# Separate buffers in the expert_v stage, and a recurrent scan issued by pairs of heads

## The chip, the cores and the metric

The kernel runs on one core of one Trainium2 chip. The metric is the device time of one execution in microseconds (us). Three runs of the kernel before took 2474.93, 2481.82 and 2487.04 us. The engines are TensorE (PE, with PEld for its weight loads), VectorE (DVE), ScalarE (ACT), GpSimd (POOL) and SyncE (SP), each of which works through its own instructions in order; SP and POOL also issue the DMA transfers.

## What is computed

The reference runs two transformer blocks over one sequence of 512 tokens with 1024 features, in fp32. Cut to what matters here:

```
# first block, mixer: 4 heads of a gated delta rule, 4 heads of sparse attention
for c in 8 chunks of 64 tokens:                       # per head, state 128x128
    v_new = u[c] - w[c] @ state
    o[c]  = q_dec[c] @ state + a[c] @ v_new
    state = state * g_last[c] + k_dec[c].T @ v_new
o_n = attention(q, compressed / selected / window keys)  # in blocks of 128 queries
x = x + gate1 * concat(o_g, o_n) @ w_out              # then a gated feed-forward layer

# second block, last part: 16384 experts, each one row of expert_u and of expert_v
experts, gate = top 16 of 16384 for each token and each of 8 heads
act = gelu(expert_u[experts] . h)
x = x + gate2 * sum(gate * act * expert_v[experts])
return rmsnorm(x, final_g)
```

## The kernel before

One program in which a scheduler orders each engine's instructions from the order in which they are written (their priority), from buffers that come free and from an estimate of durations; the order is then fixed. Every tile name has a number of buffers; a new tile of a name waits until the oldest is released by all its readers, and a pool that is opened takes memory that earlier pools give up, so its tiles wait for these. The large matrix products run on float32r operands that are split in two: `split` (L192 to L194) casts a tile to a high part on ScalarE and subtracts it on VectorE for the low part, and three products (high times high, high times low, low times high) are summed in PSUM.

**First block** (`block1`, from L401). After gates, keys and the inverse of each head's triangular matrix, the loop over the four heads projects q and v (`proj_qv`: a product with 24 matmuls of 512 columns for each, a causal convolution on VectorE, a norm) and finishes the head's scan inputs (`gdn_fin`, PSUM bank 0). Attention blocks 0 and 1 (`nsa`, 128 queries each, all four heads) are written behind heads 0 and 1. Then follows the scan (`gdn_scan`, L738): 8 steps over 64 tokens, all four heads in a step. A step takes the state times w into PSUM bank 0, subtracts on VectorE (L753), multiplies with the keys into bank 1, scales and adds the state on VectorE (L759, L760), and makes the outputs in bank 0 again (two products of 64 columns per head, each of which the trace shows as two records), which ScalarE copies out (L765). Behind the scan are written the four gate projections (`proj_gz`) and attention blocks 2 and 3. A block with `last` false uses banks 2 and 3 for scores, 4 for transposes and bank 1 for its outputs (L896); with `last` true it uses the accumulation banks, 2 to 5. The attention outputs are copied at L907.

**Second block, last part** (`peer`, L1057). The tokens fall into two shares. For the first 384, all 16384 experts are computed densely, 128 at a time: the U stage multiplies expert_u tiles with the normed input (`run_ahead`), applies gelu and writes the activations of 113 of the 128 tiles to DRAM (`spill`). A routing stage and a spreading stage (`spread`) build the gate table, 11 of 12 parts in DRAM (`gdram`) and the last in memory (`glast`); U products fill in beside them. For the last 128 tokens, the 128 (head, choice) slots are gathered instead: one indirect DMA on POOL fetches a row of expert_u or expert_v for each token, 512 KB in all, and VectorE forms a dot product (L1181) or adds up (L1191).

The **last stage** (V, L1121 to L1161) loops over the 128 expert tiles: load the activations back (`pact`, 4 buffers, SP), multiply by the gate table (`gtile`, 4 tiles to a load of 704 KB; L1139 for 11 parts, L1140 for the last), split them (`pwh`, `pwl`), load 512 KB of expert_v (`raw`, SP), split it (`vh`, `vl`, 4 pairs in a pool that is opened with this stage), then gather and add one slot (`gather_sum(1)`), then 24 matmuls of 384 columns into 8 banks. The last three tiles are done together at the end. `ulane` is a ring of 6 `row` buffers with 3 split pairs, made for expert_u; in this stage the V tiles use its 6 buffers, and so do the gathers (`self.row = ulane[0]`, L1112). Of the 128 gathers, the first are issued in the spreading stage, so the last tiles have none.

Of the kernel before, what the change touches and what calls it, by code (L numbers as in the profile page):

```python
# [9 lines left out]
F32 = mybir.dt.float32  # L10
F32R = mybir.dt.float32r
# [139 lines left out]
class Builder:  # L151
# [248 lines left out]
    def block1(self):  # L400
        A, V, x = self.A, self.V, self.x  # L401
        with ExitStack() as st1:
# [55 lines left out]
            with ExitStack() as st2:  # L458
# [15 lines left out]
                self.nsa_begin(kp)  # L474
                for h in range(4):
                    self.proj_qv(h, hi, lo)
                    self.gdn_fin(h)
                    if h < 2:
                        self.nsa(kp, h, False)
                self.gdn_scan()  # L480
                for h in range(4):
                    if h % 2:
                        self.nsa(kp, 2 + h // 2, True)
                    self.proj_gz(h, hi, lo)
            hst.close()
# [234 lines left out]
    def gdn_fin(self, h):  # L720
# [3 lines left out]
        psq = self.ps(0)  # L724
# [7 lines left out]
        ps = self.ps(0)  # L732
# [5 lines left out]
    def gdn_scan(self):  # L738
        V, C, gi = self.V, self.C, self.gi
        wT, at, qd, kd = self.wT, self.at, self.qd, self.kd  # L740
        St = gi.tile([P, 4, P], F32, name="w0", bufs=2)
        V.memset(St, 0.0)
        oT = self.eq
        for c in range(8):
# [4 lines left out]
            psv = self.ps(0)  # L749
            for h in range(4):  # L750
                self.mm(psv[:, h * P:(h + 1) * P], wT[h][:, tb], St[:, h, :])
            vnew = gi.tile([P, 4, P], F32, name="w1", bufs=2)
            V.tensor_tensor(vnew[r], self.kA[r, :, tb], psv[r].rearrange("p (h d) -> p h d", h=4), ALU.subtract)  # L753
            if c < 7:
                psS = self.ps(1)
                for h in range(4):
                    self.mm(psS[:, h * P:(h + 1) * P], kd[h][r, t, :], vnew[r, h, :])
                Sn = gi.tile([P, 4, P], F32, name="w0", bufs=2)
                V.tensor_tensor(Sn, St, self.gl[:, c, :].unsqueeze(2).to_broadcast([P, 4, P]), ALU.mult)  # L759
                V.tensor_tensor(Sn, Sn, psS.rearrange("p (h d) -> p h d", h=4), ALU.add)  # L760
            pso = self.ps(0)
            for h in range(4):
                self.mm(pso[:, h * P:h * P + 64], St[:, h, :], qd[h][:, cs], True, False)
                self.mm(pso[:, h * P:h * P + 64], vnew[r, h, :], at[h][r, t, o:o + 64], False, True)
            C.copy(oT[:, :, cs], pso.rearrange("p (h b) -> p h b", h=4)[:, :, 0:64])  # L765
            if c < 7:
                St = Sn
        self.oT = oT
# [574 lines left out]
```

## Time and profile before

| what | value |
|---|---|
| runs | 2474.93, 2481.82, 2487.04 us |
| profiled execution | 2477.21 us, span 2475.1 us |
| TensorE busy | 2378.9 us, 96%, 12749 matmuls |
| TensorE weight loads | 2150.7 us, 87% |
| VectorE, ScalarE, GpSimd busy | 1843.3 us (74%), 1077.1 us (44%), 337.5 us (14%) |
| TensorE clock granted, mean | 0.977 |
| DMA | 509.40 MB, mean 206 GB/s; 134.23 MB of it indirect (GpSimd's queue) |
| chain of waits by engine | PE 58%, DVE 13%, DMA 13%, issue 7%, ACT 6%, POOL 2% |

Matmuls are pipelined and their ends are modelled, so TensorE shown as busy is not TensorE at its peak: a stretch at half clock is also "busy". What a stage could gain is therefore read from the number of matmuls that it gets through, its clock, and the waits that interrupt it. "issue" in the chain is time without a wait that the profile shows.

### The profile page before, as it was taken

How to read it: one execution, taken by the hardware profiler on the slowest of the kernel's cores; microseconds unless marked ns; L12 is line 12 of the kernel's file. 1: busy time of each engine (PE TensorE's matmuls, PEld its weight loads, DVE VectorE, ACT ScalarE, POOL GpSimd, SP SyncE). 2: the span in 40 equal slices, each digit the busy share in tenths (PEclk: the TensorE clock that was granted, in tenths of full speed). 3: DMA queues.
4: the chain of work that ended last, by engine and by line, in shares of the span. 5: the costliest groups of instructions: out<-in, count | busy, mean ns of one | idle time of the engine just before them, and what ended most of it. 6: DMA issues, size and time to landing. Idle time of an engine off the chain costs nothing.

```text
span 2475.1 us, 35106 instructions
## 1 busy us (share of the span) xinstructions
PE 2378.9 (96%) x12749; PEld 2150.7 (87%) x12749; DVE 1843.3 (74%) x3826; ACT 1077.1 (44%) x1753; POOL 337.5 (14%) x284
## 2 busy tenths in 40 slices
PE   7999999899999999998999999999998999899998
PEld 7788787678878777877899999999998999899997
DVE  6774635788874389665999999899876777787764
ACT  4534624343332233334323334499995333333332
POOL 0000000000000000000232331233101222223310
PEclk9999989899999999998999999999998999999999
DMA  7341102566554222225478897689867999899981
GB/s 276 125 133 60 52 9 85 170 198 193 188 183 144 81 90 92 70 86 188 148 239 291 319 369 259 202 320 345 321 228 244 301 312 311 301 330 327 325 266 52
DMA packets 197934, 509.40 MB, mean 206 GB/s; under 512 B 20352, under 2 KB 93312, under 8 KB 195840
## 3 DMA queue, kind: packets, MB, share of 16 engines
q1 hardware_dynamic: 160896, 372.92, 44.4%
q0 software_dynamic: 36864, 134.23, 15.3%
q8 instruction: 100, 1.64, 0.3%
q14 instruction: 74, 0.61, 0.1%
HBM read 459.71 MB, written 47.38 MB: 205 GB/s over the span
## 4 chain that ended last, share of the span: by engine, by line
PE 58%; DVE 13%; DMA 13%; issue 7%; ACT 6%; POOL 2%; POOLq 0%; DVEq 0%; SPq 0%; ACTq 0%
PE p L162 38%; PE acc L162 19%; DMA row<-in_ev_dram,eidx 7%; DMA raw<-in_ada_dram 2%; ACT o L1296 1%; POOL row L1174 1%; ACT gstage L1304 1%; DVE grow L1181 1%; DVE pN L1191 1%; DVE wlo L194 1%; DMA araw<-in_ada_dram 1%; DVE vl L194 1%; DMA pact<-spill 1%; ACT rowhi L193 1%; DVE rowlo L194 1%
## 5 line engine op out<-in xcount | busy, mean ns | idle before, releaser
L193 ACT CAST whi<-raw 128x1024 fp32r<-128x1024 f32 (+2 forms) x152 | 150.7, 993 | 386.7 <-PE p L162 239.1
L162 PE MATMUL p<-pwl,vh 128*128 128x384 f32 x768 | 262.7, 342 | 25.0 <-DVE pwl L194 24.5
L162 PE MATMUL p<-pwh,vh 128*128 128x384 f32 x768 | 258.3, 338 | 5.2 <-ACT pwh L193 5.2
L162 PE MATMUL p<-pwh,vl 128*128 128x384 f32 x768 | 259.2, 338 | 0.0
L194 DVE TENSOR_TENSOR wlo<-raw,whi 128x1024 fp32r<-128x1024 f32 (+2 forms) x152 | 174.8, 1151 | 102.9 <-ACT whi L193 100.5
L193 ACT CAST vh<-row 128x1024 fp32r<-128x1024 f32 x128 | 134.3, 1051 | 257.3 <-PE acc L162 186.1
L1174 POOL DMA_INDIRECT row<-in_ev_dram,eidx x128 | 161.1, 1259 | 501.5 <-DVE pN L1191 188.4
L1191 DVE SCALAR_TENSOR_TENSOR pN<-row,dots,pN 128x1024 f32<-128x1024 f32 x127 | 162.7, 1281 | 84.9 <-DMA row<-in_ev_dram,eidx 84.6
L193 ACT CAST rowhi<-row 128x1024 fp32r<-128x1024 f32 x128 | 134.5, 1051 | 206.4 <-PE acc L162 94.6
L194 DVE TENSOR_TENSOR rowlo<-row,rowhi 128x1024 fp32r<-128x1024 f32 x128 | 155.8, 1218 | 35.6 <-ACT rowhi L193 35.5
L162 PE MATMUL p<-hi,rowhi 128*128 128x384 f32 x512 | 174.6, 342 | 3.2 <-ACT hi L301 2.6
L162 PE MATMUL p<-lo,rowhi 128*128 128x384 f32 x512 | 175.5, 343 | 1.8 <-DVE lo L302 1.8
L162 PEld LDWEIGHTS p<-pwl,vh 128*128 128x128 f32 x768 | 146.0, 190 | 35.8 <-DVE pwl L194 35.6
L162 PE MATMUL acc<-lo,rowhi 128*128 128x384 f32 x512 | 175.2, 342 | 0.0
L162 PE MATMUL acc<-hi,rowlo 128*128 128x384 f32 x512 | 174.8, 342 | 0.3 <-DVE rowlo L194 0.3
L162 PE MATMUL acc<-hi,rowhi 128*128 128x384 f32 x512 | 174.5, 341 | 0.6 <-ACT rowhi L193 0.6
L162 PE MATMUL p<-hi,rowlo 128*128 128x384 f32 x512 | 174.9, 342 | 0.1
L194 DVE TENSOR_TENSOR vl<-row,vh 128x1024 fp32r<-128x1024 f32 x128 | 155.9, 1219 | 24.7 <-ACT vh L193 24.7
L162 PE MATMUL p<-hi,whi 128*128 128x512 f32 x416 | 164.8, 402 | 5.7 <-ACT hi L301 4.3
L162 PE MATMUL p<-hi,wlo 128*128 128x512 f32 x416 | 166.8, 401 | 1.1 <-DVE wlo L194 1.0
L162 PE MATMUL p<-lo,whi 128*128 128x512 f32 x416 | 165.6, 399 | 0.9 <-DVE lo L302 0.9
L162 PEld LDWEIGHTS p<-pwh,vh 128*128 128x128 f32 x768 | 145.8, 190 | 5.6 <-ACT pwh L193 5.5
(525 smaller groups left out, 6055.0 us busy)
## 6 DMA issues: line engine op xcount, KB each, us to landing
row<-in_eu_dram SPq DMA_DIRECT2D x128, 512.0 KB
row<-in_ev_dram SPq DMA_DIRECT2D x128, 512.0 KB
araw<-in_ada_dram SPq DMA_DIRECT2D x64, 512.0 KB
raw<-in_up_dram SPq DMA_DIRECT2D x44, 512.0 KB
gdram<-gstage SPq DMA_DIRECT2D x11, 2048.0 KB
gtile<-gdram SPq DMA_DIRECT2D x31, 704.0 KB
spill<-pact SPq DMA_DIRECT2D x113, 192.0 KB
pact<-spill SPq DMA_DIRECT2D x113, 192.0 KB
```

Of the source, the lines that this page charges most:

```text
L162: self.T.matmul(out, lhsT, rhs, start=start, stop=stop)
L193: self.C.copy(hi, src)
L194: self.V.tensor_tensor(lo, src, hi.bitcast(F32), ALU.subtract)
L1174: self.G.indirect_dma_start(out=u, out_offset=None, in_=self.A[src], in_offset=bass.IndirectOffsetOnAxis(ap=self.eidx[:, s:s + 1], axis=0))
L1181: self.V.scalar_tensor_tensor(u, u, 1.0, self.hN, ALU.mult, ALU.mult, accum_out=self.dots[:, s:s + 1])
L1191: self.V.scalar_tensor_tensor(self.pN, v, w, self.pN, ALU.mult, ALU.add)
L1296: C.activation(o2[:, i, :], self.iota, AF.Abs, bias=T3[:, 1, t:t + 1])
L1304: C.copy(gs[:, :, q * 4:q * 4 + 4].rearrange("p a t -> p t a"), ps.rearrange("p (t a) -> p t a", t=4))
```

## The change

In the last stage the gathered rows get a name and 6 buffers of their own (`grow`), the V tiles keep the ring of 6, and the spilled activations come into 6 new buffers (`vact`) instead of 4 (`pact`) shared with the U stage. The split V weights rotate through the U stage's three pairs and one new pair, four as before. In the first block the scan is called for heads 0 and 1 behind their projections, and for heads 2 and 3 behind theirs; a step's v product, state product and outputs all lie in bank 0 (two halves), and `gdn_fin` moves to bank 4. All four attention blocks are written behind the second scan, each after one gate projection.

```diff
@@ -472,16 +472,14 @@
                 self.proj_nq(hi, lo)
                 kp = self.pool(st2, "nt")
                 self.nsa_begin(kp)
+                for pair in ((0, 1), (2, 3)):
+                    for h in pair:
+                        self.proj_qv(h, hi, lo)
+                        self.gdn_fin(h)
+                    self.gdn_scan(pair)
                 for h in range(4):
-                    self.proj_qv(h, hi, lo)
-                    self.gdn_fin(h)
-                    if h < 2:
-                        self.nsa(kp, h, False)
-                self.gdn_scan()
-                for h in range(4):
-                    if h % 2:
-                        self.nsa(kp, 2 + h // 2, True)
                     self.proj_gz(h, hi, lo)
+                    self.nsa(kp, h, h > 1)
             hst.close()
             op = self.pool(st1, "op", side="right")
             mh = self.mh = op.tile([P, KD, S], F32R, name="mh")
@@ -721,7 +719,7 @@
         V, C = self.V, self.C
         r4 = lambda v: v.rearrange("p a b -> p (a b)")
         q, k, vN, E, X = self.qT[h], self.kT[h], self.vN[h], self.at[h], self.X[h]
-        psq = self.ps(0)
+        psq = self.ps(4)
         for t in range(TT):
             b = slice(t * P, (t + 1) * P)
             self.mm(psq[:, b], k[:, b], q[:, b])
@@ -729,43 +727,45 @@
         V.tensor_tensor(q, q, self.eq[:, h, :], ALU.mult)
         self.qd.append(q)
         V.tensor_tensor(vN, vN, self.rn[:, h, :].unsqueeze(2).to_broadcast([P, TT, P]), ALU.mult)
-        ps = self.ps(0)
+        ps = self.ps(4)
         for t in range(TT):
             self.mm(ps[:, t * P:(t + 1) * P], X[:, t, :], vN[:, t, :])
         C.copy(k, ps)
 
 
-    def gdn_scan(self):
+    def gdn_scan(self, pair):
         V, C, gi = self.V, self.C, self.gi
         wT, at, qd, kd = self.wT, self.at, self.qd, self.kd
-        St = gi.tile([P, 4, P], F32, name="w0", bufs=2)
+        h0 = pair[0]
+        hs = slice(h0, h0 + 2)
+        new = lambda k: gi.tile([P, 4, P], F32, name=f"w{k}", bufs=2)[:, 0:2, :]
+        St = new(0)
         V.memset(St, 0.0)
-        oT = self.eq
+        oT = self.oT = self.eq
+        half = lambda ps, i: ps[:, i * 2 * P:(i + 1) * 2 * P]
         for c in range(8):
             t, o = divmod(c * 64, P)
             r = slice(o, o + 64)
             tb = slice(t * P, (t + 1) * P)
             cs = slice(c * 64, c * 64 + 64)
-            psv = self.ps(0)
-            for h in range(4):
-                self.mm(psv[:, h * P:(h + 1) * P], wT[h][:, tb], St[:, h, :])
-            vnew = gi.tile([P, 4, P], F32, name="w1", bufs=2)
-            V.tensor_tensor(vnew[r], self.kA[r, :, tb], psv[r].rearrange("p (h d) -> p h d", h=4), ALU.subtract)
+            ps = self.ps(0)
+            psv, psS = half(ps, 0), half(ps, 1)
+            for i, h in enumerate(pair):
+                self.mm(psv[:, i * P:(i + 1) * P], wT[h][:, tb], St[:, i, :])
+            vnew = new(1)
+            V.tensor_tensor(vnew[r], self.kA[r, hs, tb], psv[r].rearrange("p (h d) -> p h d", h=2), ALU.subtract)
             if c < 7:
-                psS = self.ps(1)
-                for h in range(4):
-                    self.mm(psS[:, h * P:(h + 1) * P], kd[h][r, t, :], vnew[r, h, :])
-                Sn = gi.tile([P, 4, P], F32, name="w0", bufs=2)
-                V.tensor_tensor(Sn, St, self.gl[:, c, :].unsqueeze(2).to_broadcast([P, 4, P]), ALU.mult)
-                V.tensor_tensor(Sn, Sn, psS.rearrange("p (h d) -> p h d", h=4), ALU.add)
-            pso = self.ps(0)
-            for h in range(4):
-                self.mm(pso[:, h * P:h * P + 64], St[:, h, :], qd[h][:, cs], True, False)
-                self.mm(pso[:, h * P:h * P + 64], vnew[r, h, :], at[h][r, t, o:o + 64], False, True)
-            C.copy(oT[:, :, cs], pso.rearrange("p (h b) -> p h b", h=4)[:, :, 0:64])
+                for i, h in enumerate(pair):
+                    self.mm(psS[:, i * P:(i + 1) * P], kd[h][r, t, :], vnew[r, i, :])
+                Sn = new(0)
+                V.tensor_tensor(Sn, St, self.gl[:, c, hs].unsqueeze(2).to_broadcast([P, 2, P]), ALU.mult)
+                V.tensor_tensor(Sn, Sn, psS.rearrange("p (h d) -> p h d", h=2), ALU.add)
+            for i, h in enumerate(pair):
+                self.mm(psv[:, i * P:i * P + 64], St[:, i, :], qd[h][:, cs], True, False)
+                self.mm(psv[:, i * P:i * P + 64], vnew[r, i, :], at[h][r, t, o:o + 64], False, True)
+            C.copy(oT[:, hs, cs], psv.rearrange("p (h b) -> p h b", h=2)[:, :, 0:64])
             if c < 7:
                 St = Sn
-        self.oT = oT
 
     def gdn_out(self):
         V, C, G, gp, oT = self.V, self.C, self.G, self.gp, self.oT
@@ -1122,6 +1122,9 @@
                 bank = [self.ps(m) if m < 6 else self.acc() for m in range(KD)]
                 self.sqp = (wk, 4)
                 part = []
+                pair = lambda: [wk.tile([P, D], F32R, name=n, bufs=1) for n in ("vh", "vl")]
+                vring = ulane[1] * LAST + [pair]
+                self.row = lambda: wk.tile([P, D], F32, name="grow", bufs=6)
                 for e in range(P):
                     if e == 0 or e % GA == 2:
                         n, e0 = min(GA, P - e) if e else 2, e
@@ -1131,7 +1134,7 @@
                             gt = self.hN[:, :(NB - 1) * n * TB].rearrange("p (b a t) -> p b a t", b=NB - 1, a=n)
                         self.dma(gt, gd[:, :, e:e + n, :].rearrange("b p a t -> p b a t"))
                     if e < KEPT:
-                        act = ra.tile([P, ND], F32, name="pact", bufs=4)
+                        act = wk.tile([P, ND], F32, name="vact", bufs=6)
                         self.dma(act, sp[e])
                     else:
                         act = kept[e]
@@ -1143,8 +1146,8 @@
                     self.split(wh, wl, act)
                     raw = ulane[0]()
                     self.dma(raw, A["ev"][e * P:(e + 1) * P, :])
-                    vh = wk.tile([P, D], F32R, name="vh", bufs=LAST + 1)
-                    vl = wk.tile([P, D], F32R, name="vl", bufs=LAST + 1)
+                    vring.append(vring.pop(0))
+                    vh, vl = vring[-1]()
                     self.split(vh, vl, raw)
                     part.append((e, wh, wl, vh, vl))
                     self.gather_sum(1)
```

## Rows read from the trace of the kernel before

**Rows 1.** The page's chain of waits, share of the span by engine and line.
```profile
...
PE p L162 38%; PE acc L162 19%; DMA row<-in_ev_dram,eidx 7%; DMA raw<-in_ada_dram 2%; ACT o L1296 1%; POOL row L1174 1%; ACT gstage L1304 1%; DVE grow L1181 1%; DVE pN L1191 1%; DVE wlo L194 1%; DMA araw<-in_ada_dram 1%; DVE vl L194 1%; DMA pact<-spill 1%; ACT rowhi L193 1%; DVE rowlo L194 1%
...
```

**Rows 2.** Busy time of each engine in stretches of the last stage.
```profile
core 0: us, PE busy (x) PEld busy (x) DVE busy (x) ACT busy (x) POOL busy (x), PEclk, DMA share, GB/s
1884.00:2391.00 507.00, 482.04 (x2688) 471.15 (x2689) 379.44 (x561) 169.55 (x225) 137.04 (x106) 0.98 0.91 311
2181.00:2248.00 67.00, 67.00 (x389) 67.00 (x388) 53.55 (x80) 23.91 (x32) 17.83 (x16) 1.00 0.96 338
2391.00:2458.00 67.00, 67.00 (x391) 66.78 (x390) 35.73 (x48) 22.83 (x32) 0.00 (x0) 1.00 0.27 86
```

**Rows 3.** Waits in the last stage; us in total, times, longest us.
```profile
PE p L162 <- DVE pwl L194: 24.5, 25, 2.4
...
DVE pN L1191 <- DMA row<-in_ev_dram,eidx: 76.1, 50, 5.7
...
DVE pact L1139 <- DMA pact<-spill: 48.3, 39, 2.9
...
POOL row L1174 <- DVE pN L1191: 174.6, 58, 7.3
...
```

**Rows 4.** Busy time of each engine, first block, around the scan.
```profile
...
290.00:320.00 30.00, 26.32 (x144) 19.83 (x142) 15.39 (x53) 10.76 (x34) 0.00 (x0) 0.89 0.06 18
320.00:400.00 80.00, 80.00 (x392) 63.85 (x391) 29.20 (x74) 21.99 (x53) 0.00 (x0) 0.81 0.04 14
...
```

**Rows 5.** Busy time of each engine in the expert_u stage.
```profile
...
1420.00:1460.00 40.00, 40.00 (x230) 40.00 (x229) 40.00 (x89) 13.47 (x19) 18.00 (x15) 1.00 1.01 385
...
```

**Rows 6.** Order of time, start of the last stage; start us, us, instruction.
```profile
1870.25 0.38 SPq L1132 DMA_DIRECT2D hN<-gdram  x1
...
1874.24 0.96 DVE L1139 TENSOR_TENSOR pact<-pact,hN 128x352 f32<-128x352 f32 x2 [2.12 <-DMA hN<-gdram]
...
1878.71 1.01 ACT L1304 COPY glast<-p 128x512 f32<-128x512 f32 x1 [0.69 <-PE p L162]
...
1879.53 3.88 ACT L193 CAST vh<-row 128x1024 fp32r<-128x1024 f32 x4
...
1879.76 0.49 DVE L1140 TENSOR_TENSOR pact<-pact,glast 128x32 f32<-128x32 f32 x4 [4.56 <-ACT glast L1304]
...
1883.31 0.93 ACT L193 CAST pwh<-pact 128x384 fp32r<-128x384 f32 x2
...
1883.87 2.29 PE L162 MATMUL p<-pwh,vh 128*128 128x384 f32 x6 [5.19 <-ACT pwh L193]
...
```

**Rows 7.** Loads of spilled activations: duration ns, first and last start.
```profile
...
L1135 SPq DMA_DIRECT2D pact<-spill x113: 319/338/1537, 1769.5 to 2370.5; - x113
...
```

**Rows 8.** Order of time: one scan step (a short VectorE operation first).
```profile
313.58 0.29 DVE L888 TENSOR_TENSOR acc<-acc,cb 128x128 f32<-128x128 f32 x1
...
316.30 1.06 PE L162 MATMUL p<-w,T 128*128 128x128 f32 x8
...
317.39 0.69 DVE L753 TENSOR_TENSOR w<-kA,p 64x512 f32<-64x512 f32 x1
...
318.14 1.16 PE L162 MATMUL p<-w,kN 64*128 64x128 f32 x8 [0.79 <-DVE w L753]
...
319.22 0.43 PE L162 MATMUL p<-qA,w 128*128 128x64 f32 x2
...
319.33 0.69 DVE L760 TENSOR_TENSOR w<-w,p 128x512 f32<-128x512 f32 x1 [0.92 <-PE p L162]
...
322.24 0.37 ACT L765 COPY eq<-p 128x256 f32<-128x256 f32 x1 [6.17 <-PE p L162]
...
322.66 1.17 PE L162 MATMUL p<-w,T 128*128 128x128 f32 x4
...
```

**Rows 9.** Scan's subtractions and additions, attention's copies: first and last start.
```profile
L753 DVE TENSOR_TENSOR w<-kA,p x8: 678/686/693, 292.4 to 393.7; 64x512 f32<-64x512 f32 x8
...
L760 DVE TENSOR_TENSOR w<-w,p x7: 678/686/689, 315.3 to 385.9; 128x512 f32<-128x512 f32 x7
...
L907 ACT COPY x<-p x5: 248/266/268, 284.8 to 312.0; 128x128 f32<-128x128 f32 x5
...
```

## The prediction

> **What bounds the kernel now.** I read the chain of waits by line first. TensorE matmuls hold 57% of it, and the largest item that is not TensorE is the indirect load of expert_v rows, 7% [rows 1]. So the question is where TensorE stands still or runs slowly, and the change touches two such places.
>
> The last stage (V) is read from the table of stretches [rows 2]. An expert takes 24 matmuls. From 1884 to 2391 us, while one gathered row tile is still fetched per expert, 2688 matmuls (112 experts) take 507 us. In the fed stretch 2181 to 2248, 389 take 67 us, as fast as the stretch from 2391, where DMA has almost nothing to do (0.27). At that pace 2688 would take 67 / 389 x 2688 = 463 us, so 507 - 463 = 44 us are lost. The DMA engines are nearly as loaded: 0.91 x 507 = 461 us of work. VectorE has room: 53.6 of 67 us in the fed stretch. The table of waits says what breaks the pace [rows 3]: TensorE waits 24.5 us on the low part of the activations (pwl, VectorE), and VectorE, which works in order, waits 76.1 us for gathered rows and 48.3 us for spilled activations. The gathers themselves wait on GpSimd, 174.6 us of it until an accumulation (pN) frees a row buffer. One ring of 6 serves V weights (SP) and gathers (GpSimd), so each has about three.
>
> The first block is read the same way [rows 4]. In 290 to 400 us TensorE has a clock of 0.89 and 0.81 although it is listed busy for 106 of 110 us. With the two levels 1.2 and 2.4 GHz that is 2 x 0.11 x 30 + 2 x 0.19 x 80 = 37 us at the lower level, which cost 18.5 us of full-speed work; idle time adds 30 - 26.3 = 3.7 us.
>
> **The change, part by part.** The sum is made against the profiled execution (2477.2 us, span 2475.1); the median of the runs is 4.6 us above it, and I add that at the end.
>
> V, steady state. No instruction and no byte is added: 128 weight tiles, 128 gathers, 113 spilled tiles as before. Gathers and weights get 6 buffers each, activations 6 for 4. A gather is then issued 6 experts ahead, 6 x 4.1 = 25 us, against a longest wait of 5.7 us for one [rows 3]; a spilled tile likewise, against 2.9 us. Both VectorE waits should go, and with them TensorE's wait on pwl. On SP a spilled load that waits for its buffer still holds the weight loads queued behind it, but two experts later than now; on GpSimd nothing else is queued in this stage. What is late next is DMA itself: 461 us of work against 463 us of TensorE. The fed stretch ran at a share of 0.96 [rows 2], the expert_u stage at 1.01 for 40 us [rows 5]. I take 0.96, the same mix of transfers: 461 / 0.96 = 480 us, a gain of 27 us. Ends: 0 if the share stays 0.91, 44 us if TensorE alone decides.
> The Trainium skill (DMA: Bandwidth & Descriptors, section Specifications) gives about 358 GB/s of HBM per core; the 311 GB/s x 507 us of [rows 2] would need 440 us by it, so TensorE would decide and this part would be 44 us, the third rival below without its first-block part. The trace does not bear the figure out as a ceiling: 385 GB/s for 40 us [rows 5].
>
> V, its start. The last piece of the gate table is copied at 1878.71 + 1.01 = 1879.72; TensorE starts at 1883.87, because ScalarE first casts four V tiles (3.88 us) and then the activations [rows 6]. Three of the first four V pairs now are the expert_u stage's, free as soon as its products are done and not with the buffers of the stage between, so their casts can go into earlier gaps. What must follow the table is a product (0.49 / 4 = 0.12) and a cast (0.93 / 2 = 0.47), so about 1880.5: 3 us. Against it: the first spilled loads now go into new buffers, while the old ones were issued from 1769.5 on [rows 7]. A load issued at 1870.25 was there at 1874.24 [rows 6], so up to 1875 the wait for the table covers it; if all six had to wait for the stage's end, some 4 us would be lost instead. I take 3 us gained.
>
> First block. The scan's matmuls are the same, issued for two heads at a time. VectorE's three operations per step take 0.69 us for 512 columns; for 256 they lie between 0.29 (128 columns) and 0.69, about 0.41 [rows 8]: 16 x 3 x 0.41 = 20 us instead of 8 x 3 x 0.69 = 17, beside a VectorE busy 29 of 80 us [rows 4]. Moved: the second pair's q and v projections now stand beside the first scan, gz and all four attention blocks beside or behind the second. Their weight loads keep their order on SP, with DMA at 0.06 or less there [rows 4]. Two things go. First, the scan's state product uses PSUM bank 1, which attention block 1 holds for its outputs: the first step subtracts at 292.4 and adds its state only at 315.3, after block 1's last copy at 312.0 [rows 9]. Now nothing in the short blocks shares a bank with the scan. Second, the output products of a step (16 matmuls of 64 columns, from 319.22 to the copy at 322.24, 3.0 us in a row [rows 8]) come in halves, with 512-column projections available between; the step shown was followed by the lower level (four matmuls in 1.17 us, where eight of the kind took 1.06). Of the 18.5 + 3.7 = 22 us at stake I take 13, since the second scan still stands among attention work as now. Ends: 22 gained; 13 lost, if the scans stand alone. For that a step now runs from 316.30 to 322.66, 6.4 us [rows 8]. A step of half width is, read from the same rows, 0.6 (state into v) + 0.5 (subtract) + 0.65 (state product) + 0.5 (add) + 1.5 (outputs) + 0.3 (copy), about 4 us: 16 x 4 = 64 against 8 x 6.4 = 51.
> In that step the output products begin at 319.22 and the add reads the state product from 319.33 to 320.02 [rows 8], so they overlap; in the change both lie in one bank. By the Trainium skill (PSUM — Partial Sum Buffer, section PSUM bank collisions raise a hardware error) two engines must not be in one bank and quadrant at a time, so the outputs must wait for the add. By that rule a step is 4.0 us, without it 3.5, and 16 steps cost 8 us more, where no other work covers them; this speaks for the fifth rival.
>
> Sum: -27 - 3 - 13 = -43; 2477.2 - 43 = 2434, and 4.6 more against the median: **2439**.
>
> **Rivals.** (1) Only V gains: 2439 + 13 = 2452. For it: the scan must again share TensorE with many small attention products; against: the bank wait of 23 us has no successor.
> (2) The wait only moves: the DMA share stays 0.91 and V keeps its 507 us. Gain 3 + 13: 2466. For it: DMA work and TensorE work differ by 2 us in 460; against: shares of 0.96 and more are in the trace.
> (3) TensorE decides everywhere: -44 - 3 - 22 = -69: 2413. For it: the fed stretch lasted 16 experts with the old buffers.
> (4) The other side: more transfers side by side make each slower. The stage becomes 461 x (1 + x) / 0.98, and all is lost from x = 11% on (523 us, the 507 plus the other gains of 16); at 15% it is 541, so +34 - 16 = +18: 2500. For it: the rate at full share is 311 / 0.91 = 342 GB/s over the long stretch and 352 in the fed one, so it does vary; against: 381 (385 / 1.01) at the highest load in the trace [rows 5].
> (5) The scans stand on the path, -30 + 13 = -17: 2465. Against: 16 steps of 4 us have some 100 us of projections and attention to stand beside, provided these are ordered next to them.
>
> **Chances.** Forecast 0.42, (1) 0.14, (2) 0.12, (3) 0.16, (4) 0.06, (5) 0.10. A measurement here tells 0.5% (12 us) from no change, so "faster" ends at 2469. The forecast, (1) and (3) lie below it, (2) and (5) within 5 us of it, of which I count 0.13 as faster: 0.85. Same: the other 0.09 and a little of (4), 0.10. Slower: 0.05. The range 2415 to 2468 leaves out half of (3), all of (4) and the upper edge of (2) and (5), 0.20 together.
>
> **What would show it.** V right: VectorE's waits for gathered rows and spilled tiles fall from 124 us to under 30, 2688 matmuls in about 480 us, a DMA share of about 0.96. If the waits go and the time stays, DMA bounds (2, 4): then look at the share and the rate per share. Start: first V matmul within 1 us of the table's last copy. First block: no 23 us gap between the first subtract and the first add and lower-level time in it below 15 us. The prediction is wrong if either part's waits go without the stage getting shorter, or if the first V matmul comes later after the table than now.

## The result and the profile after

The changed kernel takes 2441.79 us (median of 4 runs, 2438.59 to 2442.5), the kernel before beside it 2481.34 us: a ratio of 0.9839 [0.9813, 0.9864]. The forecast was 2439. The profiled execution took 2441.69 us, its span 2439.8 us, 35.3 us less than before. Marks that both traces have divide these 35.3 us:

```
from ... to                                            before    after   difference
start -> first norm behind the block (nrp)               472.8    472.6     -0.2
-> next norm (feed-forward, not changed)                 380.3    377.2     -3.1
-> end of the last copy of the gate table (glast)       1026.6   1032.2     +5.6
-> first V matmul                                          4.2      3.9     -0.3
-> last V matmul                                         574.26   536.23   -38.0
-> end of the span                                        17.0     17.7     +0.7
```

So the gain is the last stage alone, and more than all of it. The chain of waits by engine and by line, to be held against [rows 1]:

```profile
PE 66%; DVE 11%; DMA 10%; ACT 7%; issue 6%; POOL 0%; POOLq 0%; SPq 0%; DVEq 0%; ACTq 0%
PE p L162 44%; PE acc L162 21%; DMA araw<-in_ada_dram 6%; DVE araw L335 2%; ACT o L1299 2%; ACT gstage L1307 1%; DMA raw<-in_ada_dram 1%; DVE grow L1184 1%; ACT rowhi L193 1%; DMA row<-in_er_dram,eidx 1%; DVE rowlo L194 1%; ACT o L1300 1%; 
```

The gathered rows of expert_v, 7% before, are gone from it. Busy time by stretch of the last stage, to be held against [rows 2], with one stretch from its start:

```profile
core 0: us, PE busy (x) PEld busy (x) DVE busy (x) ACT busy (x) POOL busy (x), PEclk, DMA share, GB/s
1886.00:2355.00 469.00, 467.55 (x2689) 467.04 (x2690) 387.02 (x569) 168.88 (x226) 120.13 (x110) 1.00 0.97 343
...
2355.00:2422.00 67.00, 67.00 (x390) 66.74 (x389) 33.05 (x45) 22.80 (x32) 0.00 (x0) 1.00 0.22 70
...
1900.00:2020.00 120.00, 120.00 (x694) 120.00 (x693) 105.95 (x152) 42.76 (x57) 44.97 (x34) 1.00 1.05 384
```

2689 matmuls take 469 us where 2688 took 507, and the pace (24 matmuls in 24 x 469 / 2689 = 4.19 us, 4.16 without the first expert, which takes 7.3) is within 1% of that of the last 67 us (24 x 67 / 390 = 4.12 us), in which hardly a transfer is left: TensorE decides from the second expert to the end. The share of 0.96 was no ceiling for the DMA engines: they ran at 1.05 for 120 us.

Behind the gate table the order of time of the changed kernel is (answers to [rows 6]):

```profile
1865.10 1.03 ACT L193 CAST rowhi<-row 128x1024 fp32r<-128x1024 f32 x1
...
1870.69 1.04 ACT L193 CAST rowhi<-row 128x1024 fp32r<-128x1024 f32 x1
...
1881.02 1.01 ACT L1307 COPY glast<-p 128x512 f32<-128x512 f32 x1 [0.68 <-PE p L162]
1881.05 0.80 SPq L1138 DMA_DIRECT2D vact<-spill  x2
...
1881.83 1.05 ACT L193 CAST vh<-row 128x1024 fp32r<-128x1024 f32 x1
...
1884.66 0.51 DVE L1142 TENSOR_TENSOR vact<-vact,hN 128x352 f32<-128x352 f32 x1
...
1885.33 1.15 ACT L193 CAST pwh<-vact 128x384 fp32r<-128x384 f32 x2 [2.45 <-DVE vact L1143]
...
1885.89 1.33 PE L162 MATMUL p<-pwh,rowhi 128*128 128x384 f32 x3 [4.92 <-ACT pwh L193]
```

Three of four V casts did move ahead of the table's end (two of them here, as rowhi), as forecast. But the first spilled loads are issued at 1881.05, while the table's last copy runs, not from 1769.5 on [rows 7], so the product waits until 1884.66 and the start comes only 0.3 us earlier behind the table than before.

The first block, stretches as in [rows 4], and then the first and last start of the scan's subtractions and additions, the attention outputs, the first operation of an attention block and the gate projections' copies, as in [rows 9]:

```profile
290.00:320.00 30.00, 29.06 (x132) 22.83 (x130) 12.24 (x39) 10.14 (x26) 0.00 (x0) 0.77 0.11 36
320.00:400.00 80.00, 76.84 (x434) 60.97 (x434) 44.73 (x153) 37.70 (x98) 0.00 (x0) 0.94 0.04 11
```
```profile
L756 DVE TENSOR_TENSOR w<-kA,p x16: 402/420/425, 259.6 to 393.3; 64x256 f32<-64x256 f32 x16
...
L762 DVE TENSOR_TENSOR w<-w,p x14: 407/420/422, 264.4 to 388.0; 128x256 f32<-128x256 f32 x14
...
L907 ACT COPY x<-p x16: 246/265/268, 311.4 to 428.9; 128x128 f32<-128x128 f32 x16
...
L864 DVE TENSOR_TENSOR sc<-p,cb x4: 291/291/292, 298.1 to 388.3; 128x128 f32<-128x128 f32 x4
...
L601 ACT COPY x<-acc x4: 577/578/582, 283.7 to 384.8; 128x512 f32<-128x512 f32 x4
```

The bank wait has gone: the first addition comes 4.8 us after the first subtraction, for 22.9. The scan ends no earlier for it (last subtraction 393.3, before 393.7): its 16 steps of two heads stand 133.7 / 15 = 8.9 us apart on average (8 steps of four heads before: 101.3 / 7 = 14.5). The forecast had 4 and 6.4 us for a step. Attention starts at 298.1 and its last output is copied at 428.9, so its four blocks stand one behind the other for 131 us. The clock is lower in the first stretch and higher in the second.

### The profile page after: what moved, and what is told of

The parts are those of the page before. It is cut to its first block, busy times and chain, and to the rows that moved or that the text cites. A ratio compares the mean times of both kernels' runs of the same rounds, so it can differ in the third digit from the quotient of the medians.

```text
span 2439.8 us, 34987 instructions
## 1 busy us (share of the span) xinstructions
PE 2367.1 (97%) x12749; PEld 2149.7 (88%) x12749; DVE 1848.3 (76%) x3849; ACT 1071.1 (44%) x1755; POOL 322.2 (13%) x284
## 4 chain that ended last, share of the span: by engine, by line
PE 66%; DVE 11%; DMA 10%; ACT 7%; issue 6%; POOL 0%; POOLq 0%; SPq 0%; DVEq 0%; ACTq 0%
PE p L162 44%; PE acc L162 21%; DMA araw<-in_ada_dram 6%; DVE araw L335 2%; ACT o L1299 2%; ACT gstage L1307 1%; DMA raw<-in_ada_dram 1%; DVE grow L1184 1%; ACT rowhi L193 1%; DMA row<-in_er_dram,eidx 1%; DVE rowlo L194 1%; ACT o L1300 1%; ACT whi L193 1%; DVE tix L1200 1%; DVE wqrlo L194 1%
## 5 line engine op out<-in xcount | busy, mean ns | idle before, releaser
L194 DVE TENSOR_TENSOR rowlo<-row,rowhi 128x1024 fp32r<-128x1024 f32 x224 | 274.1, 1224 | 128.3 <-ACT rowhi L193 123.5
L162 PE MATMUL p<-pwh,rowhi 128*128 128x384 f32 x576 | 193.0, 337 | 4.9 <-ACT pwh L193 4.9
L162 PE MATMUL p<-pwl,rowhi 128*128 128x384 f32 x576 | 192.5, 334 | 1.4 <-DVE pwl L194 1.4
L162 PE MATMUL p<-pwh,rowlo 128*128 128x384 f32 x576 | 192.5, 334 | 0.0
L1177 POOL DMA_INDIRECT grow<-in_ev_dram,eidx x112 | 123.8, 1105 | 387.9 <-DVE pN L1194 232.4
L1177 POOL DMA_INDIRECT grow<-in_er_dram,eidx x91 | 108.5, 1192 | 283.2 <-DVE rsc L1201 104.7
L1194 DVE SCALAR_TENSOR_TENSOR pN<-grow,dots,pN 128x1024 f32<-128x1024 f32 x112 | 143.0, 1277 | 2.7 <-DMA grow<-in_ev_dram,eidx 2.5
L162 PE MATMUL acc<-hi,whi 128*128 128x512 f32 x352 | 143.0, 407 | 0.0
L162 PE MATMUL acc<-lo,whi 128*128 128x512 f32 x352 | 142.1, 404 | 0.0
L162 PE MATMUL acc<-hi,wlo 128*128 128x512 f32 x352 | 141.3, 401 | 0.0
```

The source lines that it names most:

```text
L162: self.T.matmul(out, lhsT, rhs, start=start, stop=stop)
L194: self.V.tensor_tensor(lo, src, hi.bitcast(F32), ALU.subtract)
L1177: self.G.indirect_dma_start(out=u, out_offset=None, in_=self.A[src], in_offset=bass.IndirectOffsetOnAxis(ap=self.eidx[:, s:s + 1], axis=0))
L1194: self.V.scalar_tensor_tensor(self.pN, v, w, self.pN, ALU.mult, ALU.add)
```

## The experiments

The kernel before took 2487.29 us beside e1 to e4, 2483.33 beside e5 to e8 and 2482.66 beside e9 to e12. Theory: the whole gain is the last stage, and there it is the end of sharing one ring. Rivals: depth of the buffers; a share of the gain from the first block that its own troubles hide.

**The two halves.** e1 has the changed last stage (the whole of `peer`) with the first block of before; e2 the reverse.

```diff
 e1_v_only, on after (gdn_fin and gdn_scan of before as well)
-                for pair in ((0, 1), (2, 3)):
-                    for h in pair:
-                        self.proj_qv(h, hi, lo)
-                        self.gdn_fin(h)
-                    self.gdn_scan(pair)
+                for h in range(4):
+                    self.proj_qv(h, hi, lo)
+                    self.gdn_fin(h)
+                    if h < 2:
+                        self.nsa(kp, h, False)
+                self.gdn_scan()
...
 e2_block_only, on after
-                vring = ulane[1] * LAST + [pair]
-                self.row = lambda: wk.tile([P, D], F32, name="grow", bufs=6)
-                        act = wk.tile([P, ND], F32, name="vact", bufs=6)
+                        act = ra.tile([P, ND], F32, name="pact", bufs=4)
...
```

> Only the last stage is changed; the first block stays as before. If the two parts of the change add up, as the traces say (last stage -38 us, its start and the end of the stage before it +4, the first block -3): 2481 - 33 = 2448 us. Rival: part of the 38 us came from the first block's new order shifting the transfers behind it; then 2455 or more.

> Only the first block is changed. By the trace of the changed kernel the first routing gather starts 3 us earlier, so 2478 us. The forecast's term of 13 us would give 2468. Rival: the two parts hide each other, and alone this part brings 8 us or more.

e1 took 2448.05 us, 0.986 [0.9834, 0.9886], as expected; its V matmuls span 538.7 us. e2 took 2483.55 us, 0.9992 [0.9968, 1.0016]. The first block gives nothing that can be told from zero; at most 8 us lie within the interval, and the 13 us of the forecast are out.

**Gather buffers.** e5 is the kernel before with one new line; e6 is the changed kernel with two gather buffers.

```diff
 e5_gather_own3, on before
+                self.row = lambda: wk.tile([P, D], F32, name="grow", bufs=3)
 e6_gather2, on after
-                self.row = lambda: wk.tile([P, D], F32, name="grow", bufs=6)
+                self.row = lambda: wk.tile([P, D], F32, name="grow", bufs=2)
```

> The kernel before, with one edit: the gathered V rows get 3 buffers of their own, so that the V weights keep the ring of 6; spilled activations (4 buffers, shared name) and split V weights are as before. Theory (it is the separation that pays, because a gather that waits for an accumulation then no longer takes the buffer that a weight load needs): most of the last stage's 38 us, about 30 us gained, 2453 us if the kernel before takes 2483; VectorE's wait for gathered rows falls from 76 us to below 15. Rival (depth pays, 6 buffers against about 3): a gain below 10 us, 2475 us or more, with VectorE's wait for gathered rows above 50 us.

> The changed kernel, with 2 gather buffers for 6. Theory (separation): the gather of one slot still is under way while the other is added, and one takes less than two experts, 8.3 us; so as the changed kernel within 4 us, 2442 to 2446. Rival (depth): two are too few, VectorE waits for rows again, over 40 us of it, and the stage loses 20 us or more, 2462 us.

e5 took 2436.94 us, 0.9825 [0.9776, 0.9874]: the one line has the whole gain (30 us were expected), and V takes 535.7 us. e6 took 2460.54 us, 0.9908 [0.9878, 0.9939], V 555.7 us: my expectation missed and the rival (2462) was right, two are too few. What e5 does not show is that separation alone pays: with 3 + 6 it also has nine row buffers where the ring had six. A shared ring of nine, or six split into three and three, was not run.

**Activation buffers.** e9 is the kernel before with the six new activation buffers only; gathers and weights still share the ring of 6.

```diff
 e9_acts_only, on before
-                        act = ra.tile([P, ND], F32, name="pact", bufs=4)
+                        act = wk.tile([P, ND], F32, name="vact", bufs=6)
```

> The kernel before, with one edit: the spilled activations come into 6 new buffers; weights and gathered rows still share the ring of 6. Theory (VectorE's 48 us of waits for spilled tiles are not a shortage of their buffers: their loads are held on SP's queue behind weight loads that wait for the shared ring, since with own gather buffers and the old four activation buffers only 6.6 us of them were left): TensorE's time in the last stage stays above 565 us (574 before), and the time is the same within 5 us, 2478 to 2488 us if the kernel before takes 2483. Rival (the forecast's: four buffers are too few): the stage becomes 10 to 15 us shorter, 2470 us.

e9 took 2451.57 us, 0.9879 [0.9843, 0.9914], V 545.2 us. Theory and rival both fell: this edit, which leaves the shared ring alone, gains 31 us by itself (none expected by the theory, about 13 by the rival). So sharing the ring was not the whole cause either. What the two edits have in common is seen on VectorE. For four kernels follow its row of one stretch of 465 us, and behind that all that it waited there for a transfer and, in e9 and e5, for the casts of V weights (us in total, times, longest us). The kernel before:

```profile
1890.00:2355.00 465.00, 445.85 (x2501) 436.44 (x2500) 345.82 (x509) 157.39 (x207) 126.55 (x101) 0.99 0.91 313
```
```profile
DVE pN L1191 <- DMA row<-in_ev_dram,eidx: 67.5, 46, 5.7
DVE pact L1139 <- DMA pact<-spill: 48.3, 39, 2.9
```

e9, activation buffers alone:

```profile
1890.00:2355.00 465.00, 458.50 (x2623) 455.68 (x2622) 377.21 (x565) 160.62 (x220) 160.09 (x106) 0.99 0.96 339
```
```profile
DVE pN L1191 <- DMA row<-in_ev_dram,eidx: 65.8, 44, 3.5
DVE vl L194 <- ACT vh L193: 12.2, 19, 1.2
DVE vact L1139 <- DMA vact<-spill: 8.1, 8, 2.4
```

e6, two gather buffers:

```profile
1890.00:2355.00 465.00, 456.10 (x2597) 452.56 (x2596) 362.31 (x543) 158.99 (x218) 159.30 (x103) 0.99 0.93 325
```
```profile
DVE pN L1194 <- DMA grow<-in_ev_dram,eidx: 89.4, 61, 3.7
DVE vact L1142 <- DMA vact<-spill: 11.2, 10, 2.3
```

e5, three gather buffers of its own:

```profile
1890.00:2355.00 465.00, 465.00 (x2685) 465.00 (x2684) 384.18 (x566) 164.30 (x225) 117.54 (x107) 1.00 0.97 342
```
```profile
DVE vl L194 <- ACT vh L193: 73.0, 92, 1.9
DVE pact L1140 <- DMA pact<-spill: 6.6, 8, 1.9
DVE pN L1192 <- DMA grow<-in_ev_dram,eidx: 1.4, 1, 1.4
```

Add VectorE's busy time (the third of the five busy figures) and its two waits for transfers. Before: 345.8 + 67.5 + 48.3 = 461.6 of 465 us, for 2501 matmuls. e6: 362.3 + 89.4 + 11.2 = 462.9. In both VectorE had no time left, and TensorE ran at VectorE's pace. e9: 377.2 + 65.8 + 8.1 = 451.1, 14 us under the line. e5: 384.2 + 8.0 = 392.2, with 73 us to spare, and TensorE at its own pace; VectorE spends the spare time waiting for casts on ScalarE (73.0 us), which it does not do in this stretch before. The engine works in order, so its waits add up; at TensorE's pace it has 465 - 384 = 81 us for both. Before it needed 116. Each of the two edits takes 40 us or more off, and either brings the sum of the whole stretch under the line. e9's 14 us all lie late. Its row by halves, with the two waits of the first:

```profile
1890.00:2130.00 240.00, 233.79 (x1328) 231.28 (x1327) 184.46 (x279) 81.53 (x112) 96.40 (x54) 0.99 0.93 324
2130.00:2355.00 225.00, 224.72 (x1297) 224.40 (x1296) 192.75 (x286) 79.09 (x108) 63.68 (x53) 1.00 1.00 354
```
```profile
DVE pN L1191 <- DMA row<-in_ev_dram,eidx: 53.3, 34, 3.5
DVE vact L1139 <- DMA vact<-spill: 1.9, 3, 1.2
```

Up to 2130 the sum is 184.5 + 53.3 + 1.9 = 239.7 of 240 us, VectorE is still full, and TensorE gets 1328 matmuls where e5's pace gives 1386; from there on it has time left. The 58 missing matmuls are 10 us, about as much as e9's V stage is longer than e5's (545.2 and 535.7 us). The sums fit all four kernels.

e5 also shows what the wait for spilled tiles was: with the same four buffers as before it fell from 48.3 to 6.6 us. Their loads wait on SP until VectorE has split the tile that lay in the buffer; the waits of SP's queue in the same stretch, the kernel before and then e5:

```profile
SPq L1135 <- DVE pwl L194: 73.1, 52, 4.4
```
```profile
SPq L1136 <- DVE pwl L194: 22.5, 25, 1.9
```

A late VectorE made its own loads late. Four buffers were too few only for an engine that was behind.

**The start of the last stage.** e4 is the changed kernel with its first four activation tiles in the old buffers; e10 is e5 with the split V weights in the three U pairs and one new pair, as the change has them.

```diff
 e4_first_acts_old, on after
-                        act = wk.tile([P, ND], F32, name="vact", bufs=6)
+                        act = ra.tile([P, ND], F32, name="pact", bufs=4) if e < 4 else wk.tile([P, ND], F32, name="vact", bufs=6)
 e10_own3_upairs, on e5
+                pair = lambda: [wk.tile([P, D], F32R, name=n, bufs=1) for n in ("vh", "vl")]
+                vring = ulane[1] * LAST + [pair]
-                    vh = wk.tile([P, D], F32R, name="vh", bufs=LAST + 1)
-                    vl = wk.tile([P, D], F32R, name="vl", bufs=LAST + 1)
+                    vring.append(vring.pop(0))
+                    vh, vl = vring[-1]()
```

> The changed kernel, but the first four spilled activation tiles come into the old buffers, which are free long before the last stage; all others into the new ones. Theory: the start was lost because the first loads into the new pool waited for the spreading stage's memory (issued 1881.05, one copy before the stage's end; product at 1884.7); so the first V matmul comes 1 to 2 us after the gate table's last copy instead of 3.9, and the time falls by 2 to 3 us, 2439. Rival: what delays the start is ScalarE, which casts V tiles among the spreading stage's last copies; then the matmul comes no earlier and the time stays 2442.

> The kernel before, with 3 own gather buffers and the split V weights in the three U pairs and one new pair; spilled activations in the old four buffers. Steady last stage as with the 3 gather buffers alone, 536 us. Theory (the change's late start has two causes: casts of V weights between the last copies of the gate table, 4 us, and the late first spilled loads, 2.6 us): the first V matmul comes about 1.3 us after the table's last copy, but that copy stands some 4 us later, so within 3 us of the kernel with 3 gather buffers alone: 2436 to 2440. Rival (the casts cost the table nothing, the new activation buffers did): the table is not later, and 3 us are gained on it, 2433.

e4 took 2437.0 us, 0.9806 [0.9776, 0.9836]; e10 2442.92 us, 0.9834 [0.9801, 0.9867]. The traces tell more than these times. The last copy of the table and the first V matmul, e4 and then e10:

```profile
1883.33 1.01 ACT L1307 COPY glast<-p 128x512 f32<-128x512 f32 x1 [0.69 <-PE p L162]
...
1885.65 2.29 PE L162 MATMUL p<-pwh,rowhi 128*128 128x384 f32 x6 [2.36 <-ACT pwh L193]
```
```profile
1888.52 1.01 ACT L1307 COPY glast<-p 128x512 f32<-128x512 f32 x1 [0.67 <-PE p L162]
...
1890.85 2.29 PE L162 MATMUL p<-pwh,rowhi 128*128 128x384 f32 x6 [2.36 <-ACT pwh L193]
```

TensorE starts 1.3 us after the table's last copy (1885.65 - 1884.34, 1890.85 - 1889.53), where the change needs 3.9 and the kernel before 4.2. So the late spilled loads cost 2.6 us, as e4's theory had it. The table itself is later where V casts go into the U pairs: from the norm behind the feed-forward layer to the end of the table's last copy it takes 1031.9 to 1034.4 us in the eight profiles with that edit (mean 1032.9; e10 1034.2) and 1025.4 to 1029.7 in the six without (mean 1028.1; e5 1025.4), with no overlap. That is 4.8 us lost for some 3 won; e10's 2442.92 us lie just above the 2436 to 2440 of its theory, which its interval does not exclude. ScalarE's casts between the table's copies (1865.10 and 1870.69 above) are the likely cause; no run moved them alone.

**The first block.** e3 is the changed kernel with the products of `gdn_fin` in bank 5, so that attention can have bank 4 early; e7 is the kernel before with the scan's state product in bank 5 for bank 1; e8 is the changed kernel with the four gate projections behind all attention blocks.

```diff
 e3_fin5, on after (psq and ps in gdn_fin)
-        psq = self.ps(4)
+        psq = self.ps(5)
 e7_scan_bank5, on before
-                psS = self.ps(1)
+                psS = self.ps(5)
 e8_gz_last, on after
                 for h in range(4):
-                    self.proj_gz(h, hi, lo)
                     self.nsa(kp, h, h > 1)
+                for h in range(4):
+                    self.proj_gz(h, hi, lo)
```

> The changed kernel with gdn_fin's two products in PSUM bank 5 instead of 4. Theory: attention block 0 can't take bank 4 before the last head's gdn_fin has had it (written order), so its first VectorE operation came at 298 instead of 234 us and no attention work stood beside the projections; with bank 5 it comes before 245 us, the attention blocks end earlier and the kernel takes 2430 (8 to 15 us less than 2442). Rival: the two scans, one strictly behind the other (259 to 395 us), set the end; then block 0 starts early too but the time stays within 3 us of 2442.

> The kernel before, with one edit: the scan's state product lies in PSUM bank 5 for bank 1, which attention block 1 holds. Nothing else of the change. The forecast's reason (the wait of 23 us for that bank costs TensorE time): the first state is added within 6 us of the first subtraction, lower-level time in the block falls below 25 us from 37, and 6 to 10 us are gained, about 2475 us if the kernel before takes 2483. Rival, which the trace of the change speaks for (TensorE had attention and projections to work on during that wait, so the scan only moves against work that then is lacking later): the gap goes, the lower-level time stays at 30 us or more, and the time is the same within 3 us, 2480 to 2486.

> The changed kernel, with one edit: the four gate projections are written behind all four attention blocks instead of one before each. Theory (in the changed kernel three of the four gate projections are worked off at 283 to 300 us, and then from 300 to 400 us nothing dense is left to stand between the scan and attention products): they now stand in that stretch, lower-level time in 200 to 440 us falls from 34 us to below 15, and the kernel gains 8 to 12 us on the changed one: 2430 to 2434 us. Rival (the four attention blocks, 31 us each and one behind the other from 298 us on, set the end of the block): the projections move but the last attention output still is copied at about 429 us, 2442 us within 4.

e3: 2449.33 us, 0.987 [0.9835, 0.9905]. My theory of an early attention fell: block 0 starts at 229.7 for 298.1 and the last attention output is copied at 398.8 for 428.9, but the scan inputs come later (253 to 313 us for 246 to 292), the last scan output is copied at 417.3 for 395.3, and the norm behind the block comes at 476.5. The rival's 2442 us within 3 was missed as well. Bank 5 is not free either: each head's v is transposed there (L566), so whether that or the attention beside them holds the scan inputs up is not told apart.

e8: 2445.43 us, 0.9855 [0.9806, 0.9905]; the theory fell, and of the rival only the time came true. The attention outputs and the gate projections' copies, first and last start:

```profile
L908 ACT COPY x<-p x16: 254/266/276, 296.0 to 402.0; 128x128 f32<-128x128 f32 x16
...
L602 ACT COPY x<-acc x4: 573/578/581, 397.7 to 417.6; 128x512 f32<-128x512 f32 x4
```

Attention ends 27 us earlier, so it didn't set the end either (the rival), and the projections did not go between the small products but behind nearly all of them: 397.7 to 417.6. The norm comes at 471.9, as ever.

e7: 2494.81 us, 1.0047 [1.0019, 1.0075]: a little slower, which neither the theory (8 us faster) nor the rival (the same within 3 us) had. Its subtractions, additions and attention outputs, and one stretch with what TensorE did in it (matmuls, then busy us and mean ns):

```profile
L753 DVE TENSOR_TENSOR w<-kA,p x8: 669/685/692, 290.4 to 368.7; 64x512 f32<-64x512 f32 x8
...
L760 DVE TENSOR_TENSOR w<-w,p x7: 674/687/689, 292.3 to 361.1; 128x512 f32<-128x512 f32 x7
...
L907 ACT COPY x<-p x16: 243/265/277, 257.3 to 436.7; 128x128 f32<-128x128 f32 x16
```
```profile
331.00:369.00 38.00, 34.29 (x125) 28.53 (x124) 6.83 (x11) 2.06 (x5) 0.00 (x0) 0.51 0.00 0
```
```profile
L162 PE MATMUL p<-at,w 64*128 64x64 f32 x32 | 10.7, 436 | 0.0
L162 PE MATMUL p<-qA,w 128*128 128x64 f32 x31 | 10.6, 441 | 0.0
L162 PE MATMUL p<-w,T 128*128 128x128 f32 x32 | 8.1, 436 | 1.4 <-ACT eq L765 1.4
```

The wait of 23 us is gone (292.3 - 290.4 = 1.9), and the scan's last subtraction comes 25 us earlier. But now it stands alone: from 331 to 369 nearly all matmuls are the scan's, in a row with short pauses, the granted clock is 0.51, almost all of the stretch at the lower level, and a step takes 10.3 us (337.6 to 347.9) where it took 6.4 at the higher one [rows 8]. The attention that had been mixed with it comes afterwards, to 436.7 for 419.8. Over 225 to 470 us the granted clock is 0.87, and the norm behind the block comes at 480.5, both outside what the six profiles with the old block show (0.90 to 0.93, 470.0 to 476.7).

That makes e7 no clean test of the forecast's reason, because its edit brings a new bank conflict. Attention blocks 2 and 3 (`last` true) make their transposes in bank 5 (L876), and they are written behind the scan. Block 2 has its first scores at 323.67, but its transposes (L878) start only behind the scan's last addition out of that bank:

```profile
323.67 0.29 DVE L864 TENSOR_TENSOR sc<-p,cb 128x128 f32<-128x128 f32 x1 [2.26 <-PE p L162]
...
361.11 0.69 DVE L760 TENSOR_TENSOR w<-w,p 128x512 f32<-128x512 f32 x1 [2.16 <-PE p L162]
...
365.94 1.04 PE L878 MATMUL p<-ca,sc 128*32 128x128 f32 x4
```

That is 42 us, where the kernel before has 10 (312.4 to 322.1). e7 moved the conflict from block 1 to block 2; a scan without either, in the old order, was not run.

**Side by side.** The changed kernel (e11) and e5 (e12) once more, with no edit.

> The changed kernel once more, beside the kernel with 3 gather buffers alone. Theory (the whole gain is the separation; deeper rings, new activation buffers and the scan by pairs add nothing): it takes as long as that kernel or up to 6 us longer, 2438 to 2445. Rival (they add a little, and the difference seen so far is scatter): 3 to 5 us shorter than that kernel.

> The kernel with 3 own gather buffers alone once more, beside the changed kernel. Theory: 2434 to 2440, not longer than the changed kernel. Rival: 3 to 5 us longer than it.

e11: 2441.92 us, 0.9842 [0.9805, 0.9878]; e12: 2441.53 us, 0.9842 [0.981, 0.9873], 1.5 us above its theory. One line and the whole change can't be told apart; no kernel here is shown to beat the change.

## Why the prediction was right, and where it was not

The total was right to 3 us, but all three terms behind it were off, in size, in sign or altogether, and their errors cancel: that it came so close is luck. The forecast was a gain of 43 us; between the two profiled executions the steady part of the last stage brings 38.0, its start loses 5.3, the first block brings 0.2, and stretches that the change doesn't touch bring 2.4, 35.3 in all. The medians differ by 39.5.

**V, steady: 27 us forecast, 38 measured.** The mechanism was right: VectorE's waits for transfers fell from 124 us to under 8. The step that failed is "What is late next is DMA itself ... I take 0.96". DMA ran at 0.97 over the stage and at 1.05 and 384 GB/s for 120 us near its start, its listed work came to 0.97 x 469 = 455 us, and TensorE decided: rival 3 was right for this part, and the upper end of 44 was nearer. On the disputed ceiling, the trace goes with another page of the Trainium skill (Perfetto Trace Analysis, section Roofline): 358 GB/s is a core's share while both cores of a pair draw, and one alone can go to about 435. 384 GB/s fits that; no run here had a second core at work.

The forecast also gave the reason too simply. It named two separate shortages, of row buffers and of activation buffers. e5 and e9 show one budget: VectorE's waits in series, 116 us where 81 were free. Either edit brings most of the gain (31 us by the one, all of it by the other), and their gains don't add. That rows 2 and 3 had VectorE full (379 busy + 124 of waits = 503 of 507 us) stood there to be added up; I read "room" from 53.6 of 67 us in the one stretch in which TensorE was fed.

**V, start: 3 us gained forecast, 5.3 lost measured** (+5.6 - 0.3). The bound of 4 lost was named; "up to 1875 the wait for the table covers it" failed, since the loads came at 1881.05. That alone cancels the gain of 2.6 (e4). The rest, the table some 4.8 us later with the casts in the U pairs, was not in the sum: I moved the casts "into earlier gaps" and did not count what they stand in front of on ScalarE.

**First block: 13 us forecast, nothing measured.** This is the step that failed outright, and rival 1 was right for it. By the forecast's own sign ("wrong if either part's waits go without the stage getting shorter") this half was wrong. "Two things go": the bank wait went and the output products came in halves, and no time came of either. That TensorE had other work in those 23 us is seen in [rows 4] (busy for 26.3 of 30 us in 290 to 320); that they cost nothing is argued from it and from e2, and not shown by itself, since e7 put another bank conflict in the place of the one that it removed. And the change has a conflict of its own: `gdn_fin` in bank 4, where the short attention blocks work too, puts their start off from 233.6 to 298.1; without it (e3) they start at 229.7, and the kernel is no faster. The step "with 512-column projections available between" failed too: in the changed kernel the first steps stand among projections, 16 us each (subtractions at 259.6, 275.5, 291.3), three of four gate projections are used up by 300 us, and the rest of the scan has only attention for company; 310 to 320 has a clock of 0.56. The granted clock over 225 to 470 us is 0.90 to 0.93 in six profiles with the old block (mean 0.92) and 0.90 to 0.95 in five with the new (mean 0.92), and the norm behind the block comes at 470.0 to 476.7 (mean 472.8) and 468.3 to 483.1 (mean 474.9). The mark of 15 us at the lower level, in 290 to 400 us, was met by none of these five (24 to 48 us). e3 met it, with a clock of 0.95 there (some 10 us), and was no faster: its clock over 225 to 470 us is 0.94 like theirs, and its norm comes at 476.5. Reordering moved the lower clock about. An order with dense products beside every scan step was brought about neither by e3 nor by e8 and stays untried.

By the Trainium skill (PSUM — Partial Sum Buffer, section PSUM bank collisions raise a hardware error), the output products must wait for the addition in the same bank. The trace agrees:

```profile
304.17 0.42 DVE L762 TENSOR_TENSOR w<-w,p 128x256 f32<-128x256 f32 x1 [0.22 <-PE p L162]
304.65 0.43 PE L162 MATMUL p<-qA,w 128*128 128x64 f32 x2
```

The outputs begin 0.06 us after the addition's end, and in none of the 14 steps earlier than that, while in [rows 8] they overlapped it. This shows the order, which the schedule sets; what the chip would do without it was not run. The fifth rival's price of 8 us for it is not told apart from the rest of the block.

Rivals 2 and 4 are out: the share rose, and transfers side by side did not slow each other (343 GB/s at 0.97, 354 per full share, against 342 before).

## What to carry to other kernels

An engine that works in order has one budget for all of its waits: add its busy time and its waits for transfers in a stage before calling it free, stretch by stretch and not as one average, and if the sum is the stage, one wait fewer may be enough and the second buys little. A wait on a bank or buffer during which TensorE has other work need not be lost time: take it away in a small experiment before counting it, and look up first who else works in the bank that you move to (bank 5 in e7, bank 4 in the change). A cast that moves into an "earlier gap" is charged to whatever it now stands in front of on its engine.

## What the hardware showed that was not expected

- 16 DMA engines moved 384 GB/s for 120 us, at a listed share of 1.05, with indirect gathers in the mix.
- The same block, in the same order of instructions, was granted a clock between 0.90 and 0.95 over 225 to 470 us in five profiles, and its end moved from 468.3 to 483.1 us. One profile can't decide over 10 us here.
- A scan by itself, small products with pauses below 1 us (3.7 us of 38 in all), had a granted clock of 0.51 (e7, 331 to 369 us), with TensorE listed busy for 34.3 us.
